# Seven quarter products for gate and up of 18 of 22 blocks, a grouped down projection and a feed-forward in fixed order

## Chip, cores and metric

One core of one Trainium2 chip runs the kernel. The metric is the device time in microseconds of one execution, as the median of several.

## What is computed

Two layers of a bidirectional encoder over 512 tokens of width 1024. Each layer has two feed-forward half steps (SwiGLU, inner width 2816) with a token-mixing part between them, and ends with a gated embedding of the layer. The change is in the feed-forward:

```python
def rmsnorm(x, g):
    xf = x.astype(jnp.float32)
    y = xf * lax.rsqrt(jnp.mean(xf * xf, axis=-1, keepdims=True) + EPS)
    return (y * g.astype(jnp.float32)).astype(x.dtype)

def swiglu(x, w_gate, w_up, w_down):
    return (jax.nn.silu(x @ w_gate) * (x @ w_up)) @ w_down
...
x = x + 0.5 * swiglu(rmsnorm(x, g), w_gate, w_up, w_down)
```

## The kernel before

The activations lie feature-major in SBUF: `h` is eight tiles of 128 features by 512 tokens. Every fp32 product is made of three matmuls on rounded halves (`mm3`, L156 to L158): high weight by high input, high by low, low by high. The high half of a tile is a cast on ACT (L129), the low half a subtraction on DVE (L126).

Weights come in chunks of 128x1024 fp32 (512 KB) through two buffers `wraw`, loaded by SP (`stream`); ACT casts a chunk to `whi`, DVE subtracts it to `wlo`.

`ffn` runs four times (ffn1 and ffn2 of each layer). Its 22 blocks f each take a gate chunk and an up chunk: 24 matmuls of 512 columns into a PSUM bank (`blocks`), 48 for a block. `gated` then scales by `rb`, the inverse root of the mean square, applies silu and multiplies: two DVE operations on 128x512 (L310, L313), ACT's silu (L311), a cast and a subtraction. All 22 results stay in SBUF. The down projection follows for eight output tiles m, each 22 times three matmuls; each tile is flushed by DVE (L346 scales by `rb`, L347 adds to `h`), and `nxt.chunk(m)` prepares it for the next stage: `xh` on ACT (L285), `xl` on DVE (L287), its square on ACT (L187), the sum `sqacc` of squares on DVE (L188). So between two flushes lie 66 matmuls.

The norm's `rb` is made by `Norm.wide` (L208 to L228) after the first chunk of a feed-forward (the fourth of the first one): a cast and a subtraction of `sqacc`, two matmuls with ones, one scaling, and eleven more DVE operations, one after the other. In the stages after a feed-forward (`mix`, and the layer embedding `ple`) the norm goes by `Norm.tok` (L194: matmuls of `sqacc` with ones), which TensorE runs at a fixed place among the stage's own matmuls: in `mix` behind the 48 matmuls of 272 columns at L384 to L386.

The rotary tables are made by `rope_tables` in the first feed-forward after block 3 (L247 to L270): one position load, thirteen DVE operations, two sines on ACT, two more DVE operations. In `ffn` a list scheduler sets the order of every engine's instructions; in `mix` it sets those of all but TensorE, whose order is written out.

## Time and profile before

| | before |
|---|---|
| median of 3 runs | 2096.46 us (2093.41 to 2098.4) |
| profiled execution | 2097.94 us |
| its span | 2096.2 us |
| granted TensorE clock, mean | 0.995 |
| PE busy | 98% of the span, 9624 matmuls |
| DVE, ACT, POOL busy | 51%, 37%, 1% |
| DMA | 187.08 MB, mean 89 GB/s |

A row of the timeline gives an instruction's start and its duration. Matmuls are pipelined: the distance between two starts is what one costs, and the duration is longer. Where DVE's or ACT's next instruction doesn't depend on the one before, it starts some 0.1 us before that one's end.

### The profile page before, as it was taken

Reading aid. Unit: us, or ns where it says so; the run is one execution under the profiler, and the core shown is the slowest. Engines: PE = TensorE matmul, PEld = TensorE weight load, DVE = VectorE, ACT = ScalarE, POOL = GpSimd, SP = SyncE. Lnnn points to the kernel's source line nnn. Section 1 sums busy time; section 2 is a strip of 40 time slices with the busy share of each in tenths; the row PEclk is TensorE's granted clock in tenths of the full one; section 3 lists DMA queues with packets and bytes.
Section 4 is the critical chain, followed back from the end, with each engine's and each line's share of the span. In section 5 each row is a group of like instructions: output and inputs, shape, how many; then the busy total and the mean of one; then the engine's idle time right before and its main releaser. Section 6 shows DMA issues by size and latency. Waiting matters only on the chain.

```text
span 2096.2 us, 23783 instructions
## 1 busy us (share of the span) xinstructions
PE 2058.9 (98%) x9624; PEld 1685.5 (80%) x9624; DVE 1070.9 (51%) x1655; ACT 775.5 (37%) x1170; POOL 12.8 (1%) x23
## 2 busy tenths in 40 slices
PE   8999999999899999999999999999989999999997
PEld 6888888887788888888888888888877888888887
DVE  6534334577764343344854343346786634333357
ACT  4323222456633232223532232224665322222253
POOL 0000000000000000000000000000000000000000
PEclk9999999999999999999999999999999999999999
DMA  4322222221022222222232322222211222322331
GB/s 152 102 100 91 97 94 90 86 92 50 31 91 90 101 91 95 96 91 97 95 101 90 100 92 93 98 83 87 76 51 40 93 99 91 97 94 92 100 121 41
DMA packets 55150, 187.08 MB, mean 89 GB/s; under 512 B 5984, under 2 KB 9456, under 8 KB 55040
## 3 DMA queue, kind: packets, MB, share of 16 engines
q1 hardware_dynamic: 52752, 182.10, 26.3%
q10 hardware_dynamic: 2240, 3.38, 0.5%
q8 instruction: 75, 1.23, 0.2%
q14 instruction: 35, 0.29, 0.0%
q0 software_dynamic: 48, 0.09, 0.0%
HBM read 183.44 MB, written 2.10 MB: 89 GB/s over the span
## 4 chain that ended last, share of the span: by engine, by line
PE 93%; DVE 2%; ACT 2%; issue 1%; DMA 1%; POOL 0%; DVEq 0%; SPq 0%; POOLq 0%; ACTq 0%
PE ps L156 15%; PE ps L157 15%; PE ps L158 15%; PE pm L156 14%; PE pm L158 14%; PE pm L157 14%; PE ps L384 1%; PE ps L385 1%; PE ps L386 1%; PE ps L834 1%; DVE wlo L126 0%; ACT rot L477 0%; DMA gr<-in_W 0%; PE pm L194 0%; ACT whi L129 0%
## 5 line engine op out<-in xcount | busy, mean ns | idle before, releaser
L129 ACT CAST whi<-wraw 128x1024 fp32r<-128x1024 f32 (+5 forms) x347 | 354.5, 1022 | 1106.1 <-PE ps L157 493.5
L126 DVE TENSOR_TENSOR wlo<-wraw,whi 128x1024 fp32r<-128x1024 f32 (+5 forms) x347 | 413.4, 1192 | 310.1 <-ACT whi L129 299.0
L156 PE MATMUL ps<-xh,whi 128*128 128x512 f32 x864 | 343.8, 398 | 7.2 <-ACT xh L285 7.2
L158 PE MATMUL ps<-xh,wlo 128*128 128x512 f32 x864 | 341.4, 395 | 0.2 <-DVE wlo L126 0.2
L157 PE MATMUL ps<-xl,whi 128*128 128x512 f32 x864 | 340.8, 395 | 0.0
L156 PE MATMUL pm<-xh,whi 128*128 128x512 f32 x768 | 304.5, 396 | 0.0
L158 PE MATMUL pm<-xh,wlo 128*128 128x512 f32 x768 | 302.9, 394 | 0.0
L157 PE MATMUL pm<-xl,whi 128*128 128x512 f32 x768 | 302.5, 394 | 0.0
L313 DVE TENSOR_TENSOR a<-pm,t 128x512 f32<-128x512 f32 x88 | 60.7, 692 | 278.6 <-PE pm L158 276.4
L156 PEld LDWEIGHTS ps<-xh,whi 128*128 128x128 f32 x864 | 162.8, 188 | 44.8 <-ACT xh L285 8.1
L158 PEld LDWEIGHTS ps<-xh,wlo 128*128 128x128 f32 x864 | 163.1, 189 | 40.2 <-DVE wlo L126 0.9
L157 PEld LDWEIGHTS ps<-xl,whi 128*128 128x128 f32 x864 | 163.0, 189 | 38.8 <-DVE xl L287 1.2
L158 PEld LDWEIGHTS pm<-xh,wlo 128*128 128x128 f32 x768 | 144.8, 188 | 35.1
L157 PEld LDWEIGHTS pm<-xl,whi 128*128 128x128 f32 x768 | 144.7, 188 | 33.9
L310 DVE TENSOR_TENSOR t<-ps,rbc 128x512 f32<-128x512 f32 x88 | 60.7, 692 | 217.6 <-PE ps L158 217.4
L156 PEld LDWEIGHTS pm<-xh,whi 128*128 128x128 f32 x768 | 144.6, 188 | 32.9
L156 PE MATMUL pm<-ah,whi 128*128 128x512 f32 x352 | 139.3, 396 | 0.0
L156 PE MATMUL ps<-ah,whi 128*128 128x512 f32 x352 | 139.3, 396 | 0.0
L158 PE MATMUL pm<-ah,wlo 128*128 128x512 f32 x352 | 138.7, 394 | 0.0
L158 PE MATMUL ps<-ah,wlo 128*128 128x512 f32 x352 | 138.7, 394 | 0.0
L157 PE MATMUL ps<-al,whi 128*128 128x512 f32 x352 | 138.5, 393 | 0.0
L157 PE MATMUL pm<-al,whi 128*128 128x512 f32 x352 | 138.4, 393 | 0.0
(340 smaller groups left out, 2664.3 us busy)
## 6 DMA issues: line engine op xcount, KB each, us to landing
wraw<-in_W SPq DMA_DIRECT2D x317, 512.0 KB, 3.5
gr<-in_W SPq DMA_DIRECT2D x8, 512.0 KB, 4.3
wraw<-in_W SPq DMA_DIRECT2D x8, 320.0 KB, 2.8
wraw<-in_dftc SPq DMA_DIRECT2D x4, 516.0 KB, 3.5
h<-in_xT ACTq DMA_DIRECT2D x8, 256.0 KB, 3.6
wraw<-in_W SPq DMA_DIRECT2D x4, 408.0 KB, 3.1
wraw<-in_pT SPq DMA_DIRECT2D x2, 512.0 KB, 3.5
out<-h SPq DMA_DIRECT2D x2, 512.0 KB, 3.0
```

Of the source, the lines that this page charges most:

```text
L126: V.tensor_tensor(lo, x, hi.bitcast(F32), op=ALU.subtract)
L129: S.copy(hi, x)
L156: mm(o, wh, xh, start=first, stop=False)
L157: mm(o, wh, xl, start=False, stop=False)
L158: mm(o, wl, xh, start=False, stop=last)
L310: V.tensor_tensor(t, pg, st.rb, op=ALU.mult)
L313: V.tensor_tensor(a, pu, t, op=ALU.mult)
L384: mm(pn, xh, wh[:, b], start=k == 0, stop=False)
L385: mm(pn, xh, wl[:, b], start=False, stop=False)
L386: mm(pn, xl, wh[:, b], start=False, stop=k == NK - 1)
L834: nc.tensor.transpose(pt[:, c * P:(c + 1) * P], probs[hd, c][:, kt * P:(kt + 1) * P], ident)
```

## The change

Four of the 22 blocks (`PLAIN`) stay as they were. For the other 18, gate and up together are a 2x2 matrix of quarters (gate and up; first and second half of the 1024 features), the input another (halves of features, halves of tokens), and the product of the two is made of seven quarter products (Strassen's algorithm in Winograd's form) in place of eight. A quarter product is 12 matmuls of 256 columns, so a block takes 84 of these. New around them:

- Sums of input quarters, T1 to T4, once per feed-forward and for each of four pairs of feature tiles (`combined`), made during the last four plain chunks: two ACT copies with the gain, two POOL subtractions, two DVE operations, a cast and a subtraction of 128x1024.
- Sums of weight quarters, for every block: S1 and S3 (tiles `qd`) by a 256 KB load of one quarter by SP and an accumulating load of another by GpSimd, S2 and S4 (`qa`) by DVE. Each of S1, S2, S3, S4 and A22 is then cast on ACT and subtracted on DVE into a tile `pw`.
- The gating works on halves of the tokens (128x256): copies out of PSUM by ACT, multiplications by POOL (L506, L548 and in `finish`, L462), sums and splits by DVE and ACT.
- The down projection goes in five groups of 5, 5, 4, 4 and 4 blocks, each when its blocks are done. Every group flushes all eight tiles into `h`; only the last group calls `nxt.chunk`. `rope_tables` moves behind the first group of the first feed-forward.
- All engines run in program order (`manual_schedule` without a list). A planner walks the items (a product, a chunk, a piece of the down projection) with a time each, and places loads and preparations a fixed lead ahead of the item that needs them: 12 to 24 us for loads, 7 us for casts and sums. The host packs `w_down` by groups.

```diff
+H = T // 2
+PLAIN = 4
+GROUPS = (5, 5, 4, 4, 4)
+NA = max(GROUPS) + 1
+QD = 6
...
+        with tc.tile_pool(name="ap", bufs=1) as ap, tc.manual_schedule():
+            items, clock = [], [0.0]
+            def item(us, run, tasks=()):
+                items.append((clock[0], run, tasks))
+                clock[0] += us
...
+            def chunk_tasks(w, c, halves=False):
+                if (l, c) in ahead:
+                    w["hl"] = ahead.pop((l, c))
+                    return []
+                def dma():
+                    w["raw"] = wp.tile([P, CHUNK], F32, tag="wraw", name="wraw", bufs=2)
+                    nc.sync.dma_start(w["raw"], W[l, c])
+                def prep():
+                    hi = wp.tile([P, CHUNK], F32R, tag="whi", name="whi")
+                    lo = wp.tile([P, CHUNK], F32R, tag="wlo", name="wlo")
+                    for i in range(1 + halves):
+                        b = slice(i * CHUNK // (1 + halves), (i + 1) * CHUNK // (1 + halves))
+                        S.copy(hi[:, b], w["raw"][:, b])
+                    lo_of(lo, w["raw"], hi)
+                    w["hl"] = hi, lo
+                return [(12.0, dma), (7.0, prep)]
...
+            def gated(f, pg, pu):
+                t = qa()
                 V.tensor_tensor(t, pg, st.rb, op=ALU.mult)
                 S.activation(t, t, AF.Silu)
-                a = ap.tile([P, T], F32, tag="a", name="a")
-                V.tensor_tensor(a, pu, t, op=ALU.mult)
-                ah = ap.tile([P, T], F32R, tag="ah", name="ah", bufs=NF)
-                al = ap.tile([P, T], F32R, tag="al", name="al", bufs=NF)
-                split(ah, al, a)
-                acts.append((ah, al))
-            for f in range(NF):
-                ps2 = []
+                V.tensor_tensor(t, pu, t, op=ALU.mult)
+                split(*act(f), t)
...
+            def combined(i):
+                xg = tile("pw", 6, [2, T])
+                for j in range(2):
+                    S.activation(xg[:, j], h[:, i + 4 * j], AF.Copy, scale=st.g(i + 4 * j))
+                t = tile("pw", 6, [4, H])
+                (b11, b12), (b21, b22) = ((xg[:, j, 0:H], xg[:, j, H:T]) for j in range(2))
+                G.tensor_tensor(t[:, 0], b11, b12, op=ALU.subtract)
+                G.tensor_tensor(t[:, 1], b22, b12, op=ALU.subtract)
+                V.scalar_tensor_tensor(t[:, 2], t[:, 0], -1.0, b22, op0=ALU.mult, op1=ALU.subtract)
+                V.scalar_tensor_tensor(t[:, 3], t[:, 2], -1.0, b21, op0=ALU.mult, op1=ALU.subtract)
+                hi, lo = tile("th", 4, [4, H], F32R), tile("tl", 4, [4, H], F32R)
+                split(hi, lo, t)
+                Th.append(hi)
+                Tl.append(lo)
...
+                    blocks(todo[-1][1 + i], *w["hl"], st)
+                    n = 2 * f + i
+                    if n == ready:
+                        st.rb = st.norm.wide(qd)
+                    if n > ready + 1 and i:
+                        for x in todo:
+                            gated(*x)
+                        todo.clear()
+                    if n > 2 * PLAIN - 5:
+                        combined(n - 2 * PLAIN + 4)
...
-                if first and f == 3:
-                    late_constants()
-                    rope_tables()
...
+            def parts(u, src):
+                p = U[u]["w", src] = pw()
+                S.copy(p[:, 0], U[u][src])
+                lo_of(p[:, 1], U[u][src], p[:, 0])
...
+                def acc():
+                    nc.gpsimd.dma_start(U[u][name], up[:, T:2 * T] if add == "A22" else gate[:, 0:T],
+                                        accum_op=ALU.add)
+                return [(24.0, dma), (17.0, acc)] if add else [(17.0, dma)]
...
+            def sums(u):
+                d = U[u]
+                raw = d["gate"]["raw"]
+                d["S2"] = qa()
+                V.tensor_tensor(d["S2"], raw[:, 0:T], d["S1"], op=ALU.add)
+                d["S4"] = qa()
+                V.tensor_tensor(d["S4"], raw[:, T:2 * T], d["S2"], op=ALU.add)
...
+            def product(u, o, wh, wl, name, first):
+                for i, (bh, bl) in enumerate(right(name)):
+                    b = slice(i * P, (i + 1) * P)
+                    for j, (x, y) in enumerate(((wh, bh), (wh, bl), (wl, bh))):
+                        mm(U[u][o], x[:, b], y, start=first and i + j == 0, stop=i == 3 and j == 2,
+                           skip_group_check=not first)
...
+            def finish(u):
+                d = U[u]
+                S.activation(d["g2"], d["g2"], AF.Silu)
+                G.tensor_tensor(d["g2"], d["g2"], d["c22"], op=ALU.mult)
+            def finish2(u):
+                d = U.pop(u)
+                ah, al = act(u)
+                split(ah[:, h2], al[:, h2], d["g2"])
...
+            def p1(u, after=None):
+                    d["B"] = bank("ps")[:, 0:H]
+                    hi, lo = d["gate"]["hl"]
+                    product(u, "B", hi[:, 0:T], lo[:, 0:T], "B11", True)
+                    d["g1"] = small("g1")
+                    S.copy(d["g1"], d["B"])
+                    if after is not None:
+                        finish(after)
...
+            def p5(u, after=None):
+                    product(u, "E", p[:, 0], p[:, 1], "T1", True)
+                    if after is not None:
+                        finish2(after)
...
+                def prep():
+                    parts(u, "S1")
+                    sums(u)
+                return run, load(u, "S1", 0, "A22") + [(7.0, prep)]
...
+            def p2(u):
+                    product(u, "A", hi[:, T:2 * T], lo[:, T:2 * T], "B21", True)
+                    V.tensor_tensor(d["g1"], d["g1"], d["A"], op=ALU.add)
+                    G.tensor_tensor(d["g1"], d["g1"], st.rb[:, h1], op=ALU.mult)
...
+            def p6(u):
+                    product(u, "B", p[:, 0], p[:, 1], "T2", False)
+                    d["g2"] = small("g2")
+                    S.copy(d["g2"], d["B"])
...
+            def p7(u):
+                    product(u, "B", p[:, 0], p[:, 1], "T3", False)
+                    d["c22"] = small("c22")
+                    S.copy(d["c22"], d["B"])
+                    V.scalar_tensor_tensor(d["c22"], d["E"], -1.0, d["c22"], op0=ALU.mult, op1=ALU.subtract)
+                return run, load(u, "S3", 0, "A11") + [(7.0, lambda: parts(u, "S3"))]
...
+            def p4(u):
+                    product(u, "B", p[:, 0], p[:, 1], "T4", False)
+                    V.scalar_tensor_tensor(d["g1"], d["B"], -1.0, d["g1"], op0=ALU.mult, op1=ALU.mult)
+                    ah, al = act(u)
+                    split(ah[:, h1], al[:, h1], d["g1"])
...
+            def p3(u, nxt_u):
+                    product(u, "E", p[:, 0], p[:, 1], "B22", False)
+                    V.tensor_tensor(d["g2"], d["g2"], d["E"], op=ALU.add)
+                    G.tensor_tensor(d["g2"], d["g2"], st.rb[:, h2], op=ALU.mult)
+                    if nxt_u is not None:
+                        S.activation(U[nxt_u]["g1"], U[nxt_u]["g1"], AF.Silu)
...
+            def flush(m, last):
+                y = qa()
+                V.tensor_tensor(y, pys.pop(m), st.rb, op=ALU.mult)
                 V.scalar_tensor_tensor(h[:, m], y, 0.5, h[:, m], op0=ALU.mult, op1=ALU.add)
-                nxt.chunk(m)
+                if last:
+                    nxt.chunk(m)
...
+            for u in range(PLAIN, NF - 1):
+                prev = u - 1 if u > PLAIN else None
+                put(SL, p6(u))
+                put(SL, p1(u + 1, prev))
+                put(SL, p7(u))
+                put(SL, p5(u + 1, prev))
+                put(SL, p4(u))
+                put(SL, p2(u + 1))
+                put(SL, p3(u, u + 1))
+                if u == f0 + GROUPS[g]:
+                    for x in down(f0, GROUPS[g], [(m, 0, GROUPS[g]) for m in range(NK)], False):
+                        item(*x)
+                    if first and g == 0:
+                        item(0.0, late_constants)
+                        item(0.0, rope_tables)
...
+            order = [(0, 0, 2), (1, 0, 2), (2, 0, 3), (3, 0, 3), (0, 2, 4), (1, 2, 4), (2, 3, 4), (3, 3, 4)]
+            ds = list(down(f0, n, order + [(m, 0, n) for m in range(4, NK)], True))
...
+            tasks = sorted(((t0 - lead, i, fn) for i, (t0, _, ts) in enumerate(items) for lead, fn in ts),
+                           key=lambda x: x[:2])
+            for t0, run, _ in items:
+                while tasks and tasks[0][0] <= t0:
+                    tasks.pop(0)[2]()
+                run()
```

Three places on DVE's queue, in the order in which the instructions stand. The first is the start of the second feed-forward of layer 0, where `wide` makes `rbc`. Before:

```order
L126 TENSOR_TENSOR wlo<-wraw,whi 128x1024
L222 TENSOR_SCALAR na<-nv 128x512
L223 TENSOR_SCALAR rbc<-na 128x512
L225 SCALAR_TENSOR_TENSOR na<-rbc 128x512
L226 TENSOR_TENSOR na<-na,nv 128x512
L227 SCALAR_TENSOR_TENSOR rbc<-na,rbc 128x512
L225 SCALAR_TENSOR_TENSOR na<-rbc 128x512
L226 TENSOR_TENSOR na<-na,nv 128x512
L227 SCALAR_TENSOR_TENSOR rbc<-na,rbc 128x512
L126 TENSOR_TENSOR wlo<-wraw,whi 128x1024
L225 SCALAR_TENSOR_TENSOR na<-rbc 128x512
```

Now, `qd` being the buffers that `wide` shares with the weight sums:

```order
L227 SCALAR_TENSOR_TENSOR qd<-rbc 128x512
L228 TENSOR_TENSOR qd<-qd 128x512
L229 SCALAR_TENSOR_TENSOR rbc<-qd,rbc 128x512
L227 SCALAR_TENSOR_TENSOR qd<-rbc 128x512
L228 TENSOR_TENSOR qd<-qd 128x512
L229 SCALAR_TENSOR_TENSOR rbc<-qd,rbc 128x512
L227 SCALAR_TENSOR_TENSOR qd<-rbc 128x512
L228 TENSOR_TENSOR qd<-qd 128x512
L229 SCALAR_TENSOR_TENSOR rbc<-qd,rbc 128x512
L131 TENSOR_TENSOR wlo<-wraw,whi 128x1024 x3
L366 TENSOR_TENSOR qa<-ps,rbc 128x512
```

The `wlo` of the chunks that follow stood in the middle of the chain, and now stand behind it.

The second is the end of the plain chunks of the same feed-forward, where before one block follows the next:

```order
L310 TENSOR_TENSOR t<-ps,rbc 128x512
L126 TENSOR_TENSOR wlo<-wraw,whi 128x1024
L313 TENSOR_TENSOR a<-pm,t 128x512
L126 TENSOR_TENSOR wlo<-wraw,whi 128x1024
L126 TENSOR_TENSOR al<-a,ah 128x512
L310 TENSOR_TENSOR t<-ps,rbc 128x512
L126 TENSOR_TENSOR wlo<-wraw,whi 128x1024
```

Now, right behind the last plain block's gating, with the last `combined` (L380 to `tl`) and the first Strassen blocks (`qd<-qd,pw` is a low half of S1, S3 or A22, `qa<-qa,pw` one of S2 or S4):

```order
L380 SCALAR_TENSOR_TENSOR pw<-pw 128x256
L381 SCALAR_TENSOR_TENSOR pw<-pw 128x256
L131 TENSOR_TENSOR tl<-pw,th 128x1024
L131 TENSOR_TENSOR pw<-qd,pw 128x512
L436 TENSOR_TENSOR qa<-wraw,qd 128x512
L438 TENSOR_TENSOR qa<-wraw,qa 128x512
L131 TENSOR_TENSOR pw<-qa,pw 128x512
L131 TENSOR_TENSOR wlo<-wraw,whi 128x1024
L131 TENSOR_TENSOR pw<-qd,pw 128x512 x2
L436 TENSOR_TENSOR qa<-wraw,qd 128x512
L438 TENSOR_TENSOR qa<-wraw,qa 128x512
L505 TENSOR_TENSOR g_6698<-g_6698,pm 128x256
```

The preparations for the first two Strassen blocks stand in one row behind the last plain chunk's gating and sums, and the gate sum L505 of the first stands behind them.

The third is the last tiles of the down projection of the first feed-forward. Before:

```order
L126 TENSOR_TENSOR wlo<-wraw,whi 128x1024 x3
L346 TENSOR_TENSOR t<-ps,rbc 128x512
L347 SCALAR_TENSOR_TENSOR h<-t,h 128x512
L287 SCALAR_TENSOR_TENSOR xl<-h,gv,xh 128x512
L188 TENSOR_TENSOR sqacc<-sqacc,sq 128x512
L126 TENSOR_TENSOR wlo<-wraw,whi 128x816 x2
L346 TENSOR_TENSOR t<-pm,rbc 128x512
L126 TENSOR_TENSOR wlo<-wraw,whi 128x544
L347 SCALAR_TENSOR_TENSOR h<-t,h 128x512
L392 MEMSET va 128x16
```

Now:

```order
L559 TENSOR_TENSOR qa<-pm,rbc 128x512
L131 TENSOR_TENSOR wlo<-wraw,whi 128x816
L560 SCALAR_TENSOR_TENSOR h<-qa,h 128x512
L131 TENSOR_TENSOR wlo<-wraw,whi 128x544
L289 SCALAR_TENSOR_TENSOR xl<-h,gv,xh 128x512
L193 TENSOR_TENSOR sqacc<-sqacc,sq 128x512
L559 TENSOR_TENSOR qa<-ps,rbc 128x512
L560 SCALAR_TENSOR_TENSOR h<-qa,h 128x512
L289 SCALAR_TENSOR_TENSOR xl<-h,gv,xh 128x512
```

Flushes that lay 66 matmuls apart follow each other; a tile's `xl` and `sqacc` stand ahead of the next tile's flush, and from the fifth tile on nothing stands between them. The `sqacc` of the eighth tile is then followed by the norm of `mix`.

## Rows read from the trace of the kernel before

**Rows 1.** The page: engine TensorE's busy time, and the chain that ended last.

```profile
PE 2058.9 (98%) x9624; PEld 1685.5 (80%) x9624; DVE 1070.9 (51%) x1655; ACT 775.5 (37%) x1170; POOL 12.8 (1%) x23
PE 93%; DVE 2%; ACT 2%; issue 1%; DMA 1%; POOL 0%; DVEq 0%; SPq 0%; POOLq 0%; ACTq 0%
```

**Rows 2.** Windows: start:end, length, busy us of PE, PEld, DVE, ACT, POOL, clock, DMA.

```profile
1100.00:1200.00 100.00, 100.00 (x432) 80.99 (x431) 39.93 (x45) 28.57 (x36) 0.00 (x0) 1.00 0.29 95
2060.00:2080.00 20.00, 20.00 (x170) 20.00 (x169) 16.45 (x50) 10.98 (x27) 0.00 (x0) 1.00 0.16 54
```

**Rows 3.** Timeline of PE in the last embedding, matmuls of 256 columns: start, duration.

```profile
2060.73 0.28 PE L156 MATMUL pm<-xh,gh 128*128 128x256 f32 x1
...
2065.89 0.28 PE L157 MATMUL ps<-xl,gh 128*128 128x256 f32 x1
```

**Rows 4.** Timeline of DVE: the norm's chain at the second feed-forward's start.

```profile
622.66 0.69 DVE L219 TENSOR_SCALAR nv<-pm 128x512 f32<-128x512 f32 x1 [1.24 <-PE pm L217]
...
629.55 1.22 DVE L126 TENSOR_TENSOR wlo<-wraw,whi 128x1024 fp32r<-128x1024 f32 x1
...
632.13 0.69 DVE L227 SCALAR_TENSOR_TENSOR rbc<-na,rbc 128x512 f32<-128x512 f32 x1
```

**Rows 5.** Groups of ACT by line and shape: count, busy us, mean ns, idle before.

```profile
L129 ACT CAST whi<-wraw 128x1024 fp32r<-128x1024 f32 x319 | 334.3, 1048 | 1079.4 <-PE ps L157 490.1 <-issue 351.7 <-PE pm L157 207.3
L311 ACT ACTIVATE t<-t 128x512 f32<-128x512 f32 x88 | 54.8, 628 | 0.7 <-DVE t L310 0.6
...
L1059 ACT ACTIVATE sq<-h 128x256 f32<-128x256 f32 x14 | 5.6, 417 | 7.2 <-DVE h L977 5.7 <-DVE rs_y L172 1.0 <-PE pm L1012 0.5
...
L311 ACT ACT_TABLE_LOAD x4 | 5.1, 1283 | 0.1
```

**Rows 6.** Timeline of DVE at a second feed-forward's end: flush of its last tile.

```profile
985.06 0.69 DVE L346 TENSOR_TENSOR t<-pm,rbc 128x512 f32<-128x512 f32 x1 [3.45 <-PE pm L158]
985.78 0.69 DVE L347 SCALAR_TENSOR_TENSOR h<-t,h 128x512 f32<-128x512 f32 x1
986.39 1.22 DVE L126 TENSOR_TENSOR wlo<-wraw,whi 128x1024 fp32r<-128x1024 f32 x1
987.53 0.75 DVE L287 SCALAR_TENSOR_TENSOR xl<-h,gv,xh 128x512 fp32r<-128x512 f32 x1
988.19 0.68 DVE L188 TENSOR_TENSOR sqacc<-sqacc,sq 128x512 f32<-128x512 f32 x1
```

**Rows 7.** Timeline of ACT at the same place.

```profile
986.51 0.73 ACT L285 ACTIVATE xh<-h,gv 128x512 fp32r<-128x512 f32 x1 [0.59 <-DVE h L347]
```

**Rows 8.** Timeline of POOL in a mixing stage: its only kind of compute.

```profile
488.45 0.64 POOL L656 TENSOR_SCALAR_AFFINE_SELECT E<-E 128x512 f32<-128x512 f32 x1 [4.58 <-ACT E L653]
```

**Rows 9.** Timeline of DVE from the same moment on.

```profile
488.58 0.53 DVE L678 SCALAR_TENSOR_TENSOR den<-hN 128x8 f32<-128x8 f32 x1
...
492.37 0.41 DVE L685 TENSOR_TENSOR hs<-hN 128x256 f32<-128x256 f32 x1
492.70 0.68 DVE L126 TENSOR_TENSOR yl<-yf,yh 128x512 fp32r<-128x512 f32 x1
...
497.12 0.16 DVE L678 SCALAR_TENSOR_TENSOR den<-hN 128x8 f32<-128x8 f32 x1
```

**Rows 10.** The tile rope: operation, count, duration in ns (least, median, most), starts.

```profile
L263 DVE SCALAR_TENSOR_TENSOR rope<-rope x5: 683/691/692, 47.3 to 59.9; 128x512 f32<-128x512 f32 x5
```

**Rows 11.** Timeline of PE, layer 0: mixing's first matmul and the norm's.

```profile
379.93 0.29 PE L384 MATMUL ps<-whi,xh 128*128 128x272 f32 x1
...
385.99 0.95 PE L194 MATMUL pm<-ones,sqacc 128*128 128x1 f32 x8
```

**Rows 12.** Windows around TensorE's wait at 525 us, columns as in rows 2.

```profile
524.00:528.00 4.00, 1.58 (x7) 0.74 (x6) 3.97 (x11) 3.98 (x10) 0.00 (x0) 0.87 0.00 0
528.00:532.00 4.00, 4.00 (x16) 3.19 (x16) 3.19 (x6) 2.56 (x6) 0.00 (x0) 0.71 0.40 131
```

**Rows 13.** DMA issues: kind, count, KB each, median us from issue to landing.

```profile
wraw<-in_W SPq DMA_DIRECT2D x317, 512.0 KB, 3.5
```

More of the change, by code (lines that the diff above doesn't have):

```diff
@@ new lines, in plain, with run @@
+            def plain(f, i, w):
+                def run():
+                    if i == 0:
+                        todo.append((f, bank("ps"), bank("pm")))
+                    blocks(todo[-1][1 + i], *w["hl"], st)
[8 more added lines that the diff above has]
+                        combined(n - 2 * PLAIN + 4)
+                return run
@@ new lines, in ffn, with down, run @@
+            pys = {}
+            def flush(m, last):
+                y = qa()
+                V.tensor_tensor(y, pys.pop(m), st.rb, op=ALU.mult)
+                V.scalar_tensor_tensor(h[:, m], y, 0.5, h[:, m], op0=ALU.mult, op1=ALU.add)
+                if last:
+                    nxt.chunk(m)
+            def down(f0, nf, pieces, last):
+                ws = {}
+                for m, a, b in pieces:
+                    tasks, new = [], []
+                    for j in range((m * nf + a) // 8, (m * nf + b - 1) // 8 + 1):
+                        if j not in ws:
+                            ws[j] = {}
+                            tasks += chunk_tasks(ws[j], cd + f0 + j)
+                    def run(m=m, a=a, b=b):
+                        if a == 0:
+                            pys[m] = bank("pm" if m % 2 or last and m < 4 else "ps")
+                        for i in range(a, b):
+                            hi, lo = ws[(m * nf + i) // 8]["hl"]
+                            c = slice((m * nf + i) % 8 * P, ((m * nf + i) % 8 + 1) * P)
+                            mm3(pys[m], hi[:, c], lo[:, c], *acts[f0 + i], i == 0, i == nf - 1)
+                        if b == nf:
+                            flush(m, last)
+                    yield 0.7 * (b - a), run, tasks
@@ L1121, in _pack @@
                 put(f"f{n}gu", 2 * f + 1, u[f])
[L1122 to L1124 removed]
+            d = _lhs(a[f"ffn{n}_w_down"][l]).reshape(NK, P, NF, P).transpose(1, 0, 2, 3)
+            f0 = 0
+            for nf in GROUPS:
+                blk = d[:, :, f0:f0 + nf].reshape(P, nf, CHUNK)
+                for i in range(nf):
+                    put(f"f{n}d", f0 + i, blk[:, i])
+                f0 += nf
         w = a["w_in"][l]
```

120 lines of the change are left out of this document (87 added, 33 removed).

## Prediction

> **What bounds the kernel now.** I read the page's busy shares and its chain first: PE is busy 98% of the span, and 93% of the chain that ended last is PE [rows 1]. So only two things move the time: the work that PE is given, and waits that are put on it. Waits are nearly absent now. In a plain stretch of gate and up, PE is busy 100 of 100 us with 432 matmuls, while DVE has 40 us and ACT 29 us of work in them [rows 2]; a matmul of 512 columns thus costs 100/432 = 0.2315 us. The change has no other bound to remove, and it has two idle engines to lean on.
>
> **What the change takes from PE.** A plain block is 48 matmuls, 48 x 0.2315 = 11.11 us. A Strassen block is 84 matmuls of 256 columns. Their price is shown in the last embedding, where the same three-matmul pattern runs with 256 columns: from 2060.73 to 2065.89 lie 43 steps in 5.16 us, 0.120 us each [rows 3]. That is more than half of 0.2315, and the window says why: PEld, the weight load, is busy 20 of 20 us there [rows 2]. So 84 x 0.120 = 10.08 us, and a block saves 1.03 us. There are 18 blocks in each of four feed-forwards: **72 x 1.03 = 74 us saved**. Seven eighths would have been 1.39 us each, 100 us; I take 74, from the rows. The down projection keeps its matmuls.
>
> **What it puts on PE: waits.** Now every queue runs in the order written, so I follow for each place the instruction PE waits for. A dependent 128x512 step of DVE costs 0.72 us (985.06 to 985.78 [rows 6]), an independent one some 0.6; `wlo` 1.22, or 1.13 to the next start [rows 4]; 128x256 on DVE 0.41 [rows 9]; ACT's cast of 128x1024 1.05, 128x512 0.63, 128x256 0.42 [rows 5]; ACT with a gain 0.73 [rows 7]. From the end of a PE group to DVE's use I add 0.16.
>
> A, start of each feed-forward. The norm's chain ran from 622.66 to 632.82 with two `wlo` in it [rows 4], 10.16 - 2 x 1.13 = 7.9 us alone. It begins 0.66 us after the chunk behind which it stands (two matmuls with ones, 0.46, and 0.2), so `rb` is there at +8.6. In the new order the `wlo` of the next chunk but one stands behind the whole chain: +9.8. PE wants it after 0.46 + 5.56 + two matmuls 0.46 = +6.5. 3.3 us x 4 = **13 us**.
>
> B, last plain chunk. Its `wlo` stands behind the gating of the block before and one `combined`: 0.16 + 0.69 + 0.63 (cast) + 0.63 + 0.73 (two copies) + 2 x 0.41 + 1.05 + 1.13 + 1.22 = 7.1 us after that block's end, wanted at 5.56 + 0.46 = 6.0: 1.1 us, three times. In the first feed-forward three gatings come at once there, each two DVE steps, silu, a cast and a subtraction in sequence, 3.3 us, with a table load of 1.28 [rows 5] before silu: 8.0 us. Together **11 us**.
>
> C, first Strassen product with S1. Behind the last plain chunk stand L368, its cast, the last `combined` and then the low half of S1: 0.16 + 0.69 + 0.63 + 1.36 + 0.82 + 1.05 + 1.13 + 0.69 = 6.5, with hops 6.6 us. PE has one product, 1.44, and two matmuls to do until then: wanted at 1.7. 4.9 x 4 = **20 us**.
>
> D, the third product of the same block, p7. It adds into the bank that ACT must first copy out (`g2`). That copy stands behind silu of `g1`, silu behind POOL's L506, this behind DVE's L505, and L505 behind the sums and low halves of two blocks: 6.6 + 1.32 + 0.6 + 1.13 + 1.2 + 1.32 + 0.41 = 12.6, then POOL some 0.6, ACT twice 0.42: 14.0 to 14.6. PE, delayed by C, wants it at 6.6 + 1.2 + 3 x 1.44 = 12.1. 2.2 x 4 = **9 us**.
>
> E, rotary tables, once. They now stand between the first down group and the next product, and the two sines stand in ACT's queue ahead of the copy of `g2`. Fifteen DVE steps, five of 0.69 [rows 10] and most others of 0.43, are some 8.0 us in sequence, the two sines 1.27 by ACT's 128x512 in [rows 5], ahead of them the last flush 1.5 and queued halves and sums 2.7, then the copy 0.42: +13.9, wanted after two products, +2.9. **11 us** (8 if the queued halves are done early). Before, they lay beside 5.56 us chunks and cost nothing.
>
> F, end of each feed-forward. A flush costs DVE 0.72 + 0.73 until ACT starts `xh`, 0.76 for `xh`, then `xl` 0.66 and `sqacc` 0.6 to the next: 3.47 us [rows 6, 7]. Before, 66 matmuls (15.3 us) lay between two. Now eight flushes follow on 60 matmuls, 13.9 us, and the next flush stands behind `xl`, which waits for ACT. Eight take 27.8 us, up to 30 with the chunks' low halves between. After the 13.9 us PE has 6.06 us of the next stage before the norm's matmul needs the last `sqacc` (379.93 to 385.99 [rows 11]); in front of the embedding 24 matmuls, 5.6 us. So PE waits 27.3 to 30 less 19.5 to 20: 7.4 to 10.6; I take 9 before each mixing and 11 before each embedding, which has a second use of the norm: **40 us**.
>
> Waits: 13 + 11 + 20 + 9 + 11 + 40 = **104 us**.
>
> **Clock.** After a wait of some 2 us the clock was granted at 0.71 from 528 to 532, and 16 matmuls ran in 4 us where 17.3 fit [rows 12]. Some 18 of my waits are as long: 0 to 1.3 us each, 0 to 23; I take **12**.
>
> **The steady stretch.** Between two Strassen blocks runs a ring: the copy of `c22`, the sum S2, the cast and low halves, L505, POOL's product, silu, the copy of `g2`, PE's p7. In ACT's and DVE's shares to the next start: 0.31 + 0.53 + 0.31 + 1.15 (two half casts of a chunk) + 1.22 (`wlo`) + 0.42 + 0.84 (two casts) + 0.6 (low half of S3) + 0.42 (L505), POOL 0.7, then 0.42 + 0.53 + 0.42, p7 1.44 and its end 0.16: 9.5, with hops 9.6 us; PE has 10.08. No row shows POOL with two inputs; the nearest are its select of 128x512, 0.64 [rows 8], and DVE's 128x256, 0.41. Between 0 and 0.6 us a block, 68 blocks: 0 to 41; I take **10**, near the lower end since at 0.64 the ring stays under PE. The accumulating loads have no row either. A plain 512 KB load lands in 3.5 us [rows 13]; the planner issues the second 7 us after the first and 10 us before its cast, so twice that duration would still fit, and I take nothing; were it longer than 10 us, it would lengthen each block by the excess, which I count with the upper end of the ring. The bytes grow by some 54 MB on 187, at a share of 0.29 of the DMA engines [rows 2]: not a bound.
>
> **Sum.** Against the profiled execution's 2097.94 us (span 2096.2): 2098 - 74 + 104 + 12 + 10 = 2150. The median of the runs stands 1.5 lower: **2148 us**, slower by 2.5%.
>
> **Rivals.**
>
> *The chains are covered* (faster). Place: C, D and F. My price takes each round trip between DVE and ACT as lost to DVE. If the queue in front finds its inputs earlier, DVE's own share is left: in F 0.69 + 0.69 + 0.75 + 0.68 less overlaps, 2.45 x 8 = 19.6, just PE's 19.5 to 20, which gives back 38; C shrinks to some 2 us (12 back), D to nothing (9), the clock by 7. 2148 - 66 = **2082**. It decides as soon as waits, clock and ring together cost less than 74 us. For it speaks that before DVE put a `wlo` into such a gap (986.39, between L347 and `xl`); against it, that from the fifth tile on no other instruction stands between `xh` and `xl` in the new order.
>
> *POOL and DVE shut each other out* (slower still). A 128x8 step of DVE that began within POOL's select took 0.53 us, the same step without POOL 0.16 [rows 8, 9]. Each Strassen block has three POOL multiplications on the ring, and DVE is busy 7.4 of 10 us (five low halves and two sums of 0.6 to 0.66, `wlo` 1.13, six steps of 128x256 at 0.33), mostly with steps that read two SBUF inputs. If each multiplication loses or costs 0.37 to 0.6, the ring is 10.7 us and sets the pace: 68 x 0.62 = 42 in place of 10, **2180**. The Trainium skill, page "SBUF — State Buffer", section "Who interferes with whom", says that such a DVE instruction and a GpSimd instruction that reads SBUF exclude one another, the later one being blocked wholly; the two `den` rows agree with it, though with one pair only. By that rule alone the time would be this rival's.
>
> **Chances.** Forecast 0.58, between 2105 (F halved, 20 less, clock nothing, D nothing) and 2178 (clock and F at their upper ends, 17 more, the ring 13); covered 0.26; shut out 0.16. The range reaches from 2082, the middle of the covered case, to 2190. What a measurement of this kernel can tell from no change is about 0.2%, 4 us: of the covered case 0.23 falls below 2092, 0.03 within; of the forecast 0.02 within. Faster 0.23, same 0.05, slower 0.72.
>
> **What would show it.** After, 256-column matmuls at 0.120 us and Strassen blocks of 10.1 us in undisturbed stretches show the saving; 10.7 us with waits on ACT copies shows the shutting out. PE idle before the `wlo` matmuls of the second chunk (A), before `pw` matmuls once a feed-forward (C), 11 us once after the first down group (E), and 7 to 11 us before the norm's matmul (F) show the waits. I am wrong if PE idles under 70 us in all, or if the Strassen blocks run at another pace than 10.1.

## The result: slower, 2188.4 us

The changed kernel takes 2188.43 us (median of 4 runs, 2186.86 to 2190.03); the kernel before took 2097.43 us beside it. The ratio is 1.0436, with a 95% interval of 1.0416 to 1.0456: 91 us more, where the prediction had some 50 (2148). The time lies 2 us below the upper end of its range (2190) and outside the forecast's own case (2105 to 2178).

Of the page of the changed kernel, the busy times, the granted clock in 40 slices and the chain that ended last, to be held against [rows 1]:

```profile
PE 2035.9 (93%) x12216; PEld 1791.8 (82%) x12216; DVE 1565.4 (72%) x2607; ACT 1015.5 (46%) x1938; POOL 361.9 (17%) x415
PEclk9899999999999999999899999998999999999989
PE 62%; DVE 17%; ACT 10%; issue 6%; POOL 3%; DMA 1%; ACTq 0%; DVEq 0%; POOLq 0%; SPq 0%
```

PE is busy 23 us less and the span is 92 us longer. DVE, ACT and POOL are now 30% of the chain; before they were 4%. The mean granted clock is 0.966 where it was 0.995: at half clock (1.2 in place of 2.4 GHz) that is (1 - 0.966) x 2188 / 0.5 = 149 us against 21.

Who ended TensorE's waits is in the view of its waits (line that waited, what ended the wait, us in all, times, longest). The largest of the changed kernel:

```profile
PE ps L451 <- ACT g L516: 25.4, 32, 10.6
PE ps L451 <- ACT pw L415: 20.6, 4, 5.7
PE ps L669 <- DVE qa L559: 17.3, 4, 6.3
PE ps L161 <- ACT xh L287: 12.5, 4, 6.0
PE ps L163 <- DVE wlo L131: 10.8, 5, 3.4
PE ps L161 <- DVE qa L559: 9.4, 2, 5.1
PE pm L161 <- ACT whi L353: 8.8, 4, 6.1
PE pm L163 <- DVE wlo L131: 5.7, 5, 3.3
```

Of these eight, two have a counterpart in the kernel before: 0.2 us once for `wlo`, and

```profile
PE ps L156 <- ACT xh L285: 7.2, 2, 6.2
```

I took PE's timelines of both kernels apart in the same way: each matmul's distance to the next start is split into the median distance for its line and shape, the idle time before the next, and what is left, inside and outside the stretches at half clock.

| us | before | after | change | predicted |
|---|---|---|---|---|
| matmuls at their median distance | 2042 | 1965 | -77 | -74 |
| idle time of PE | 24 | 139 | +115 | +104, and 10 for the ring |
| matmuls longer, half clock | 5 | 47 | +42 | +12 |
| matmuls longer, elsewhere | 12 | 23 | +12 | 0 |
| sum | | | +92 | +52 |

The saving and the sum of the waits came as forecast. What was missing is below them: matmuls that ran longer.

The waits by place, from the same timeline:

| place | predicted | measured | single waits |
|---|---|---|---|
| A, norm's chain before `wlo` | 13 | 12.2 | 3.3, 3.4, 2.2, 3.3 |
| B, last plain chunk, first gating | 11 | 11.2 | 6.4 once, 1.6 three times |
| C, first product with S1 | 20 | 22.8 | 4.6, 4.6, 5.7, 5.7, and 0.5 behind each |
| D, p7 of the first block | 9 | 3.8 | |
| E, rotary tables | 11 | 10.6 | 10.6 |
| F, end of each feed-forward | 40 | 37.2 | 8.7 and 8.6 before mixing, 20 in the two embeddings |
| ring | 10 | 11.0 | some 0.4, 27 blocks |

These are 109 of the 115 us. The other 6 lie at places that the forecast doesn't name, mainly at the start of the first feed-forward of each layer (PE's waits for `xh` grew from 7.2 to 12.5 us); that the sum of the waits was met to 1 us is thus in part luck.

### The profile page after: what moved, and what is told of

The parts are those of the page before. It is cut to its first block, busy times and chain, and to the rows that moved or that the text cites. A ratio compares the mean times of both kernels' runs of the same rounds, so it can differ in the third digit from the quotient of the medians.

```text
span 2188.3 us, 31811 instructions
## 1 busy us (share of the span) xinstructions
PE 2035.9 (93%) x12216; PEld 1791.8 (82%) x12216; DVE 1565.4 (72%) x2607; ACT 1015.5 (46%) x1938; POOL 361.9 (17%) x415
## 3 DMA queue, kind: packets, MB, share of 16 engines
q0 software_dynamic: 20784, 37.84, 10.6%
## 4 chain that ended last, share of the span: by engine, by line
PE 62%; DVE 17%; ACT 10%; issue 6%; POOL 3%; DMA 1%; ACTq 0%; DVEq 0%; POOLq 0%; SPq 0%
PE ps L451 12%; PE ps L163 8%; PE ps L162 8%; PE ps L161 8%; PE pm L161 7%; PE pm L163 7%; PE pm L162 7%; DVE wlo L131 4%; ACT pw L415 3%; ACT whi L353 2%; DVE pw L131 2%; PE pm L451 2%; DVE qa L436 2%; POOL g L548 1%; DVE g L505 1%
## 5 line engine op out<-in xcount | busy, mean ns | idle before, releaser
L451 PE MATMUL ps<-th,pw 128*128 128x256 f32 x2304 | 450.9, 288 | 48.2 <-ACT g L516 25.4
L451 PEld LDWEIGHTS ps<-th,pw 128*128 128x128 f32 x2304 | 374.9, 194 | 59.4 <-ACT g L516 33.6
L131 DVE TENSOR_TENSOR wlo<-wraw,whi 128x1024 fp32r<-128x1024 f32 (+3 forms) x275 | 324.5, 1181 | 79.2 <-ACT whi L134 38.4
L451 PE MATMUL ps<-tl,pw 128*128 128x256 f32 x1152 | 329.4, 286 | 0.0
L353 ACT CAST whi<-wraw 128x512 fp32r<-128x512 f32 (+1 forms) x261 | 203.4, 810 | 213.4 <-DMA wraw<-in_W 109.3
L451 PEld LDWEIGHTS ps<-tl,pw 128*128 128x128 f32 x1152 | 224.1, 195 | 0.9
L131 DVE TENSOR_TENSOR pw<-qd,pw 128x512 fp32r<-128x512 f32 x216 | 148.1, 687 | 10.9 <-ACT pw L415 5.9
L506 POOL TENSOR_TENSOR g<-g,rbc 128x256 f32<-128x256 f32 x72 | 72.5, 1007 | 387.4 <-DVE g L505 387.4
L161 PE MATMUL ps<-xh,whi 128*128 128x512 f32 x288 | 119.8, 416 | 15.7 <-ACT xh L287 12.5
L163 PE MATMUL ps<-xh,wlo 128*128 128x512 f32 x288 | 118.2, 410 | 10.8 <-DVE wlo L131 10.8
L162 PE MATMUL ps<-xl,whi 128*128 128x512 f32 x288 | 118.0, 410 | 1.2 <-DVE xl L289 1.1
```

Source lines behind the costliest of these rows:

```text
L131: V.tensor_tensor(lo, x, hi.bitcast(F32), op=ALU.subtract)
L161: mm(o, wh, xh, start=first, stop=False)
L162: mm(o, wh, xl, start=False, stop=False)
L163: mm(o, wl, xh, start=False, stop=last)
L353: S.copy(hi[:, b], w["raw"][:, b])
L451: mm(U[u][o], x[:, b], y, start=first and i + j == 0, stop=i == 3 and j == 2, skip_group_check=not first)
```

## The places in the trace of the changed kernel

A: DVE and PE at the start of the second feed-forward, as in [rows 4]. The chain's last step, then the `wlo` of two chunks, and the matmul that waited for the first:

```profile
669.92 0.69 DVE L229 SCALAR_TENSOR_TENSOR rbc<-qd,rbc 128x512 f32<-128x512 f32 x1
670.53 2.35 DVE L131 TENSOR_TENSOR wlo<-wraw,whi 128x1024 fp32r<-128x1024 f32 x2
```

```profile
671.80 0.50 PE L163 MATMUL ps<-xh,wlo 128*128 128x512 f32 x1 [3.35 <-DVE wlo L131]
```

C: DVE in the same feed-forward from the last plain chunk's gating to S1's low half, and PE:

```profile
710.42 0.69 DVE L368 TENSOR_TENSOR qa<-pm,qa 128x512 f32<-128x512 f32 x1 [0.94 <-PE pm L163]
711.79 0.69 DVE L131 TENSOR_TENSOR al<-qa,ah 128x512 fp32r<-128x512 f32 x1 [0.69 <-ACT ah L134]
713.22 0.93 DVE L380 SCALAR_TENSOR_TENSOR pw<-pw 128x256 f32<-128x256 f32 x1 [0.74 <-POOL pw L378]
714.19 0.42 DVE L381 SCALAR_TENSOR_TENSOR pw<-pw 128x256 f32<-128x256 f32 x1
715.77 1.23 DVE L131 TENSOR_TENSOR tl<-pw,th 128x1024 fp32r<-128x1024 f32 x1 [1.17 <-ACT th L134]
716.92 0.69 DVE L131 TENSOR_TENSOR pw<-qd,pw 128x512 fp32r<-128x512 f32 x1
```

```profile
716.32 0.58 PE L451 MATMUL ps<-th,pw 128*128 128x256 f32 x1 [4.60 <-ACT pw L415]
717.66 0.80 PE L451 MATMUL ps<-th,pw 128*128 128x256 f32 x2 [0.55 <-DVE pw L131]
726.02 0.39 PE L451 MATMUL ps<-th,pw 128*128 128x256 f32 x1 [1.16 <-ACT g L516]
```

The last row is D: 1.2 us, where 2.2 was forecast.

E: ACT behind the first down group. It stood idle 20 us for the last DVE step ahead of the sines, and PE stood behind its copy:

```profile
151.60 0.63 ACT L268 ACTIVATE rope<-rope 128x512 f32<-128x512 f32 x1 [20.38 <-DVE rope L266]
152.26 0.63 ACT L269 ACTIVATE rope<-rope 128x512 f32<-128x512 f32 x1
152.80 0.35 ACT L516 COPY g<-ps 128x256 f32<-128x256 f32 x1
```

```profile
153.20 0.58 PE L451 MATMUL ps<-th,pw 128*128 128x256 f32 x1 [10.63 <-ACT g L516]
```

F: DVE at the end of the first feed-forward, one tile's flush up to the next, to be held against [rows 6], and PE:

```profile
410.58 0.69 DVE L559 TENSOR_TENSOR qa<-ps,rbc 128x512 f32<-128x512 f32 x1
411.30 0.69 DVE L560 SCALAR_TENSOR_TENSOR h<-qa,h 128x512 f32<-128x512 f32 x1
412.78 0.75 DVE L289 SCALAR_TENSOR_TENSOR xl<-h,gv,xh 128x512 fp32r<-128x512 f32 x1 [0.79 <-ACT xh L287]
413.45 0.68 DVE L193 TENSOR_TENSOR sqacc<-sqacc,sq 128x512 f32<-128x512 f32 x1
414.05 0.68 DVE L559 TENSOR_TENSOR qa<-pm,rbc 128x512 f32<-128x512 f32 x1
```

```profile
411.32 0.39 PE L669 MATMUL ps<-whi,xh 128*128 128x272 f32 x1 [2.41 <-DVE qa L559]
418.26 0.60 PE L669 MATMUL ps<-whi,xh 128*128 128x272 f32 x1 [6.29 <-DVE qa L559]
```

410.58 to 414.05 is 3.47 us, the forecast distance to the hundredth. PE waited in another place than I had put it: not at the norm's matmul for `sqacc`, but for PSUM banks that the late flushes hadn't read yet.

The half clock: windows behind this wait (start:end, length, busy us of PE, PEld, DVE, ACT, POOL, clock, DMA):

```profile
420.00:424.00 4.00, 4.00 (x19) 4.00 (x19) 3.84 (x9) 1.45 (x3) 0.75 (x1) 0.50 0.00 0
424.00:428.00 4.00, 4.00 (x35) 4.00 (x34) 2.77 (x9) 1.05 (x1) 0.00 (x0) 1.00 0.05 11
```

Without any idle time PE started 19 matmuls in four microseconds at half clock and 35 in the next four; the 35 are not all of the same kind.

## Experiments

Each kernel is the changed one with the edit shown, unless said otherwise. Gains stand against 2188.4.

### Flushes without ACT's xh between them

```diff
-                if last:
+                if last and m:
+                    nxt.chunk(m - 1)
+                if last and m == NK - 1:
                     nxt.chunk(m)
```

> The changed kernel with one edit: in the last down group a tile's xh, xl and sqacc are written behind the flush of the next tile, so that DVE no longer stands behind ACT's xh between two flushes. The flushes followed each other at 3.47 us and TensorE waited 33 us for them in the four ends (2.4 and 6.3 at the first), with 15 us more at the half clock in the windows behind. Theory (the chain through ACT sets the distance): a flush costs DVE's own 2.6 us, plus the low halves of four chunks, so some 22 us of the waits go and 8 to 12 of the clock's: 2188 - 32 = 2156, between 2148 and 2166. Rival (DVE's own work or PSUM banks bound the end): waits stay, 2183 to 2190. Rival (the clock falls for other reasons than the waits): only 22 us go, 2166.

2161.79 us, 26.6 gained (ratio to before 1.0307, 1.0292 to 1.0323), within the theory's range. DVE's queue at the same place:

```profile
411.36 0.69 DVE L559 TENSOR_TENSOR qa<-ps,rbc 128x512 f32<-128x512 f32 x1
412.08 0.69 DVE L560 SCALAR_TENSOR_TENSOR h<-qa,h 128x512 f32<-128x512 f32 x1
412.69 0.75 DVE L289 SCALAR_TENSOR_TENSOR xl<-h,gv,xh 128x512 fp32r<-128x512 f32 x1
413.35 0.69 DVE L193 TENSOR_TENSOR sqacc<-sqacc,sq 128x512 f32<-128x512 f32 x1
413.95 0.69 DVE L559 TENSOR_TENSOR qa<-pm,rbc 128x512 f32<-128x512 f32 x1
```

The distance is 2.59 us. One wait of 3.0 us is left before the first mixing stage in place of 2.4 and 6.3. So most of F was ACT's round trip inside DVE's queue: by place its waits fell from 37.2 to 15 us. What is left of the distance is DVE's own four steps.

### Rotary tables in pieces

In `rope_tables` five `yield` statements, one of them taken twice, cut the row into seven pieces:

```diff
+                    rope = rope_tables() if first and g == 0 else None
                     for x in down(f0, GROUPS[g], [(m, 0, GROUPS[g]) for m in range(NK)], False):
                         item(*x)
+                        if rope:
+                            item(0.0, lambda r=rope: next(r, None))
                     if first and g == 0:
                         item(0.0, late_constants)
-                        item(0.0, rope_tables)
```

> The changed kernel with one edit: the rotary tables are written in pieces of some three DVE operations between the flushes of the first down group, in place of one row behind it. Theory (one row of DVE operations and the sines in front of ACT's copy): the single wait of 10.6 us goes and with it 2.1 us at the half clock behind it: 2188 - 12.7 = 2175.5, between 2173 and 2179. Rival (the work only moves and makes the flushes or the chunks' low halves of the down group late): under 4 us gained, 2184 to 2190.

2179.49 us, 8.9 gained, the runs between 2175 and 2183. The wait for L516, 25.4 us in 32 with one of 10.6, became 15.9 us in 32 with none over 1.4. The wait is gone and nothing took its place there; the gain came out 0.5 us under the theory's least.

### Sums of input quarters earlier

```diff
-                    if n > 2 * PLAIN - 5:
-                        combined(n - 2 * PLAIN + 4)
+                    at = (1, 2, 4, 6)
+                    if n in at:
+                        combined(at.index(n))
```

> The changed kernel with one edit: the sums of input quarters (combined) are made in the chunks 1, 2, 4 and 6 of the plain blocks in place of 4 to 7, so that none stands behind the last plain chunk's gating. Theory (the chain through combined makes the first product with S1 wait 4.6 to 5.7 us in each feed-forward, 20.6 in all, 2.2 more for the next and 9 us at the half clock behind it): the S1 low half comes 2.9 us after the last plain chunk, wanted at 1.7, so 16 us of waits go, the wait before the last plain chunk shrinks by some 4, the clock's part by 6: 2188 - 26 = 2162, between 2156 and 2172. Rival (the loads and accumulating loads of S1 set the entry, not combined): under 5 us gained.

2162.44 us, 26.0 gained, as forecast: the loads don't set the entry. The wait for ACT's `pw` fell from 20.6 to 4.6 us. D came up behind it: the waits for L516 rose from 25.4 to 32.0. D is now 2.6 us in each feed-forward: C had hidden what I had forecast there and not found. B shrank with C, from 11.2 to 3.5 us.

### The second chunk's preparation ahead of the norm's chain

```diff
-            def chunk_tasks(w, c, halves=False):
+            def chunk_tasks(w, c, halves=False, lead=7.0):
...
-                return [(12.0, dma), (7.0, prep)]
+                return [(max(12.0, lead + 5.0), dma), (lead, prep)]
...
-                    tasks = chunk_tasks(w, cgu + 2 * f + i)
+                    tasks = chunk_tasks(w, cgu + 2 * f + i, lead=12.0 if 2 * f + i == ready + 2 else 7.0)
```

> The changed kernel with one edit: the preparation of the second chunk after the norm's chain is placed ahead of the chain (lead 12 us in place of 7). Theory (in the written order that low half stands behind the whole chain): the four waits of 3.3, 3.4, 2.2 and 3.3 us go and the 6.0 us at the half clock behind them; rb comes some 2.4 us later, which the three gatings of the first feed-forward feel once: 2188 - 16 = 2172, between 2168 and 2177. Rival (rb itself is then the late one in each feed-forward, since the chain is pushed back): the waits move to the gating, 2184 to 2192.

2173.33 us, 15.1 gained, within the theory's range. The first gating paid for the later `rb`: PE's wait for `whi` there went from 6.1 to 8.9 us.

### Multiplications on DVE

The edit shown, and the same at L462 and L548:

```diff
-                    G.tensor_tensor(d["g1"], d["g1"], st.rb[:, h1], op=ALU.mult)
+                    V.tensor_tensor(d["g1"], d["g1"], st.rb[:, h1], op=ALU.mult)
```

> The changed kernel with the three multiplications of a Strassen block moved from POOL to DVE; POOL keeps its accumulating loads. In the trace of the changed kernel these take 0.73 us at the least and 1.1 at the median, and a sum of DVE that meets one takes 1.23 in place of 0.69; 28 of 72 Strassen blocks run some 0.6 us longer than 10.08, waiting for ACT's copy of g2, 16 us in all. Theory (POOL and DVE shut each other out on the ring): the ring loses 0.7 us or more at L506 and the 0.54 of the sum, DVE gains 1.0 of work a block; the waits of the steady blocks go, 12 to 16 us, and the entry of each feed-forward gains 0 to 4: 2188 - 15 = 2173, between 2168 and 2178. Rival (the ring is bound by DVE's own work): more work on DVE makes the blocks longer, 0.3 to 1.0 us in 68: 2208 to 2255.

2164.48 us, 23.9 gained, more than the theory's 15 and past its range. First the changed kernel, DVE and POOL in a Strassen block:

```profile
194.31 0.69 DVE L131 TENSOR_TENSOR pw<-qd,pw 128x512 fp32r<-128x512 f32 x1
194.91 1.23 DVE L436 TENSOR_TENSOR qa<-wraw,qd 128x512 f32<-128x512 f32 x1
```

```profile
194.47 1.12 POOL L506 TENSOR_TENSOR g<-g,rbc 128x256 f32<-128x256 f32 x1 [5.52 <-DVE g L505]
```

POOL's product started while DVE ran and took 1.12 us, to 195.59; DVE's sum started within it and took 1.23, to 196.14. From the end of the instruction in front (195.00 and 195.59), that leaves 0.59 and 0.55 us for each of them. PE's waits 10.7 us apart in that stretch:

```profile
186.16 0.39 PE L451 MATMUL ps<-th,pw 128*128 128x256 f32 x1 [0.39 <-ACT g L516]
196.88 0.38 PE L451 MATMUL ps<-th,pw 128*128 128x256 f32 x1 [0.43 <-ACT g L516]
```

With the products on DVE, the sum L436 by source line (least, median, most in ns), and PE's waits for L516:

```profile
L436 DVE TENSOR_TENSOR qa<-wraw,qd x72: 682/684/689, 85.5 to 2035.9; 128x512 f32<-128x512 f32 x72
```

```profile
PE ps L451 <- ACT g L516: 11.7, 3, 10.6
```

Before the edit the median of L436 was 1227 ns. The 32 waits became three, one of them E's; D's went with the ring's, from 3.8 us to 1.1. PE's idle time fell by 15 us, the time that matmuls ran longer outside the half clock by 8.

### More matmuls in the wait

```diff
-                        for i in range(a, b):
+                        for i in list(range(a, b)) * (3 if last and m == NK - 1 else 1):
```

> The changed kernel with the last output tile's 12 matmuls of the last down group made three times over (the first two passes are thrown away), 24 matmuls or 5.56 us more for TensorE in each feed-forward, at the place where it waits 33 us in all for flushes. It asks what the time at the half clock (152 us in the trace of the changed kernel, matmuls longer by 47 us in it) hangs on. Theory (it follows the waits): the added work lies in the waits, the last flush waits for DVE anyway, and some of the 15 us lost in the windows behind comes back: 2188 - 6, between 2176 and 2190. Rival (the clock does not follow the waits, and the added work is hidden): 2188 to 2190 with the half clock in the same windows. Rival (the added work delays the last flush): up to 2210.

2181.46 us: 22 us more matmuls, and 7 us less time. PE's idle time fell by 21 us, so the added matmuls lay in the waits. The mean granted clock rose from 0.966 to 0.974, and PE's matmuls were longer by 38 us at half clock in place of 47; at the four ends, where they were added, by 10 in place of 17. So the clock's part there belongs to the waits, and comes back as far as they are filled. At the other places this wasn't tried by itself.

### The order without the seven products

```diff
-PLAIN = 4
-GROUPS = (5, 5, 4, 4, 4)
-NA = max(GROUPS) + 1
-QD = 6
+PLAIN = 22
+GROUPS = (22,)
+NA = 22
+QD = 4
...
+                if first and f == 3:
+                    item(0.0, late_constants)
+                    item(0.0, rope_tables)
...
+            for x in down(0, NF, [(m, a, b) for m in range(NK) for a, b in ((0, 8), (8, 16), (16, NF))], True):
```

> The fixed order without the seven products: all 22 blocks plain, the down projection in one group as in the kernel before (weights packed as before), rotary tables in one row after block 3, every engine in written order with the planner. It separates the order from the algorithm. Theory (the written order alone costs what the prediction gave for A, B and the rotary tables): four waits of 3.3 us, 8 in the first gating, 4 to 8 for the tables, half clock behind them 8: 2097 + 32 = 2129, between 2115 and 2140. Rival (a fixed order with preparations 7 us ahead costs nothing by itself, all waits come from the Strassen parts): 2097 to 2103.

2136.66 us, 1.0177 of before (1.0156 to 1.0197). The written order alone costs 38 us, within the theory's range. Its largest new waits are four at A and one behind the rotary tables:

```profile
PE ps L163 <- DVE wlo L131: 10.2, 4, 3.3
...
PE ps L161 <- ACT whi L353: 3.4, 1, 3.4
PE pm L163 <- DVE wlo L131: 3.3, 1, 3.3
```

The wait for `whi` at L353 is for a cast that stood behind the two sines in ACT's queue (sines at 81.32 and 81.98 us, the cast at 82.52, PE's matmul at 83.60). At the first gating, where the theory had 8 us, PE didn't wait. By the split used above, idle time grew by 22 us, where the theory had 25 to 29, and the matmuls at half clock by 17, where it had 8. So the products, with all that they need, make 2137 into 2188: 77 us of matmuls saved and 129 paid.

### Four edits together, and the way back below before

> The four edits that were made alone (flushes without ACT's xh between them, rotary tables in pieces, sums of input quarters earlier, the second chunk's preparation ahead of the norm's chain) in one kernel. Alone they gave 26.6, 8.9, 25.9 and 15.1 us. Theory (waits at separate places, each with its own clock window): they add up to 77, 2188 - 77 = 2112, between 2104 and 2120. Rival (the waits take each other's place): 2125 to 2150. Rival (fewer waits also keep the clock up elsewhere): below 2100, which would be as fast as the kernel before.

2117.58 us: 70.8 gained of the 76.6 that the four gave alone, nearly additive. Then with the products on DVE:

> The four edits that were made alone and the multiplications on DVE, all five in one kernel. The four together came to 2117.6, the multiplications alone gave 24 us. Theory (separate places): 2117.6 - 24 = 2094, between 2088 and 2100, as fast as the kernel before. Rival (with the entry moved forward, DVE's added work is the late one there): 2100 to 2110.

2093.63 us, 0.9977 of before (0.9968 to 0.9986): another 24.0, and faster than before by 0.2%. By the same split, 50 us of idle time, 17 at half clock and 6 of other longer matmuls still stand against the 77 saved.

Two more kernels went for the waits that were left. The first:

```diff
-GROUPS = (5, 5, 4, 4, 4)
+GROUPS = (4, 4, 4, 5, 5)
...
-                    if n > ready + 1 and i:
-                        for x in todo:
-                            gated(*x)
-                        todo.clear()
-                    at = (1, 2, 4, 6)
+                    if n in ((4, 5, 6, 7) if first else (2, 3, 5, 7)):
+                        gated(*todo.pop(0))
+                    at = (0, 1, 2, 5) if first else (1, 2, 4, 6)
...
-                    tasks = chunk_tasks(w, cgu + 2 * f + i, lead=12.0 if 2 * f + i == ready + 2 else 7.0)
+                    tasks = chunk_tasks(w, cgu + 2 * f + i, lead=12.0)
...
-            order = [(0, 0, 2), (1, 0, 2), (2, 0, 3), (3, 0, 3), (0, 2, 4), (1, 2, 4), (2, 3, 4), (3, 3, 4)]
+            order = [(0, 0, 3), (1, 0, 3), (2, 0, 4), (3, 0, 4), (0, 3, 5), (1, 3, 5), (2, 4, 5), (3, 4, 5)]
```

> The five edits and three more, aimed at what TensorE still waited for in the kernel with four: each plain block is gated in a chunk of its own (4.9 us once, at the first gating), all plain chunks are prepared 12 us ahead (1.5, 0.5 and 0.7 us in each of three feed-forwards), and the last down group has five blocks (60 matmuls after the first flush become 75; 3.0 us in each of four ends). Theory (the remaining waits go one by one with their clock windows): 5 + 8 + 12 of waits and some 6 of clock, not all of it: 2094 - 22 = 2072, between 2062 and 2086, faster than the kernel before. Rival (the waits move to the next chunk): 2088 to 2098.

2089.68 us, 0.9960 of before (0.9948 to 0.9973), 4 gained of 22: the rival's time. In the profiled executions, which took nearly the same time here (2093.91 and 2093.78 us), PE's idle time fell by 9 us against the kernel with five edits, and the matmuls at half clock got 7 us longer. The chunk for the first product now came late, 3.0 us in the first feed-forward. With that chunk and S1 prepared 12 us ahead too:

```diff
-                return run, chunk_tasks(U[u]["gate"], cgu + 2 * u, True)
+                return run, chunk_tasks(U[u]["gate"], cgu + 2 * u, True, 12.0 if u == PLAIN else 7.0)
...
-                return run, load(u, "S1", 0, "A22") + [(7.0, prep)]
+                early = 5.0 if u == PLAIN else 0.0
+                return run, [(x + early, y) for x, y in load(u, "S1", 0, "A22") + [(7.0, prep)]]
```

> The kernel with eight edits and one more: the chunk and the sums for the first Strassen product of a feed-forward are prepared 12 us ahead in place of 7 (loads 5 us earlier too), since with eight edits TensorE waited 3.0, 1.2, 0.7 us in the first feed-forward and 1.0, 1.4, 1.5 in the others for this chunk's casts and for S1, which stood behind the last plain block's gating, with a half clock of 7 to 10 us behind each. Theory: 16 us of waits go, up to 8 of the clock: 2089.7 - 16 = 2074, between 2068 and 2080. Rival (the preparations only change places with the last plain chunks', whose chunks then come late): 2084 to 2092.

2089.90 us, 0.9962 (0.9948 to 0.9975): the rival, in another place. The waits for the chunk's casts fell from 1.9 to 4.2 us in each feed-forward to 0.8 once; those for S1 stayed, 0.8 to 2.0 us. PE then stood before p6 and p7 of the same first block as well, 1.5 to 3.0 and 1.9 us in each feed-forward: the waits moved on along the queues. The best kernels here are thus 0.4% faster than the one before; the 77 us of matmuls are still paid back nearly whole.

## Why the prediction held, and where its size failed

- **Matmuls**: right. 84 x 0.120 was borne out by the blocks' 10.0 to 10.1 us wherever nothing waited; 77 in place of 74.
- **A, B, C, E, F**: right in mechanism and in size, each within 3 us. A and E, and most of C and F, went by an edit each, and B shrank with the edit for C. In B two misses cancel: 6.4 for 8.0 at the first gating, 1.6 for 1.1 at the three others. In F the place of the wait was wrong (PSUM banks in mixing, not `sqacc`), which the sum didn't feel, since the same chain of flushes sets both.
- **D**: too large, 3.8 for 9. The C wait, 0.8 us longer in each feed-forward than forecast, covered part of it; with C nearly gone it was there, 2.6 us each.
- **The ring and the rival "POOL and DVE shut each other out"**: the lock is real, and I priced it on the wrong side of the forecast. I took POOL at 0.6 to 0.7 us; it took 0.73 at the least and 1.1 at the median, and the ring was 10.7 us as the rival said. But it set the pace in 27 blocks (the expectation above says 28), not in 68: the first two or so blocks behind every down group ran at 10.0 to 10.1, as if the queues had got ahead there (argued, not tested). So its cost was 11 us of idle time and some 8 of longer matmuls, between the forecast's 10 and the rival's 42. The Trainium skill, page "SBUF — State Buffer", section "Who interferes with whom", has the mechanism: of a DVE instruction with two SBUF inputs and a GpSimd instruction that reads SBUF, the later waits for the whole of the earlier. The rows of L506 and L436 agree with it, each ending 0.55 to 0.59 us behind the one in front. The Trainium skill, page "GPSIMD Engine Reference", section "3.1 Elementwise — side-by-side cycle accounting", says that an addition of two fp32 operands of 2048 elements takes about twice DVE's time on GpSimd. Here it is 0.73 us to DVE's 0.41 at 256. An estimate by that page of the Trainium skill, twice the 0.41 of [rows 9], is 0.8 us; with it the ring would have been some 9.7 us, still under PE's 10.08, so it is the blocking that was missing from the sum, and not POOL's own price.
- **The clock is the step that failed**: 12 us taken, 0 to 23 as bounds, 42 measured. I read its price from one wait of 2 us [rows 12] and gave each of 18 waits at most 1.3 us. That reading is wrong in its unit: 16 matmuls where 17.3 fit are 1.3 matmuls, or 0.3 us, and the sum took them as 1.3 us. By the split used above, the matmuls behind that wait ran 1.6 us longer, so the 1.3 came near it by luck. The second error is that the row was the cheapest case. Of 21 stretches at half clock in the changed kernel, three have a counterpart in the kernel before; the other 18, as many as forecast, lost 43 us, 2.4 each where I had taken 0.7. The cheapest lost 1.4 to 1.6. Behind 10.6 us of rotary tables the matmuls lost 2.1 us, behind the first feed-forward's end 2.6, and where two waits followed each other, in the embeddings, 4.6 and 4.8. The time at half clock was 149 us, some 7 for each stretch. The Trainium skill, page "TensorE: Matmul & The Clock Gate", section "What's actually happening", says that the throttled clock is the default and activity releases it. The kernel with more matmuls in the wait agrees, with a mean granted clock of 0.974 for 0.966.
- **The rival "the chains are covered"** didn't come true. It needed DVE's own work to be left of each flush; the edit that wrote it so gave 26.6 us.
- **The range** held, but by little, and not through its own case: the forecast's case ended at 2178 with 23 us at most for the clock, and the range reached on to 2190, beyond the rival's 2180. The lower end of the forecast's case is 2107 by its own terms (2148 - 20 - 12 - 9), not 2105, on which nothing rests.

## What to carry over

Where every engine runs in written order, a low half that stands behind a chain of ten dependent steps, or a next flush behind another engine's round trip, is a wait that could be priced here to within a few microseconds from rows of the kernel before; an algorithm that saves 9% of its blocks' matmul time (1.03 of 11.11 us) has to be worth more than these. Price a wait of TensorE of some microseconds with the half clock behind it: here 1.4 to 3.2 us for most, up to 4.8 where two waits follow each other, and none behind the ring's waits of 0.4 us. Count time and matmuls apart when reading that price from a row. Elementwise work moved to an idle POOL was not free for DVE (1.23 us for 0.68 at L436): put the dependent steps of a ring on one of the two.
